# The gated units of a last FFN by one level of Strassen's algorithm: seven half-size products in place of eight

## The chip, the cores and the metric

The kernel runs on one core of a Trainium2 chip. The metric is the device time of one execution in microseconds (us); the time before is the median of three runs. A profiled execution of the same program gives the trace: the instructions of each engine with start and length. The engines are PE (matrix multiplication; PEld is its weight load), DVE (vector), ACT (scalar functions and copies), POOL (the second vector engine) and SP, which issues the DMAs. SBUF is the on-chip memory; PSUM holds PE's sums.

## The reference, cut to what matters

The reference runs two layers over 512 latent tokens, D_MODEL 1024. Layer 0 mixes by latent attention, layer 1 by an S5 state-space layer with a GLU; each is followed by a SwiGLU FFN with 2816 hidden units. Only the last lines of layer 1 matter here: the FFN's input product, its gate, and the output product.

```python
def modulate(x, g, shift, scale):
    return rmsnorm(x, g) * (1 + scale) + shift

def swiglu(h, w_in, w_out):
    a, b = jnp.split(h @ w_in, 2, axis=-1)
    return (jax.nn.silu(a) * b) @ w_out
...
        xl = xl + gt_l * yl
        xl = xl + gt2_l * swiglu(modulate(xl, norm_ffn[i], sh2_l, sc2_l), ffn_w_in[i], ffn_w_out[i])
```

`sh2_l`, `sc2_l` and `gt2_l` are modulation rows, a product of SiLU(c) with `ada_w`.

## The kernel before, in words

**Layout and passes.** Activations stand feature-major: a tile is 128 partitions by KT = 8 chunks of k by 512 tokens. Each fp32 operand is split in two: a high part (`wh` of a weight, `hh` of the data), which ACT copies out in PE's fp32r format (L77), and a low part (`wl`, `hl`), which DVE subtracts (L80). A product is three passes for each k chunk: high by high, high weight by low data, low weight by high data (`passes`, L818).

**The FFN of layer 1** (`ffn(1, …)`, L852 and on). The 2816 hidden units are 22 tiles of 128, called units here. `BLOCKS[1]` puts them in three blocks: units 0 to 7, 8 to 14, 15 to 21. For each unit, `linear` makes two 128 x 512 accumulators, one for a and one for b: 8 chunks by 3 passes of 512 columns each, 48 matmuls in all. ACT makes `sa` = silu(a) (L873), DVE `u` = b x `sa` (L874), and `split` turns u into `uh` (ACT) and `ul` (DVE). Behind the units of a block stand eight output products `fo`, one for each chunk of the output, whose k chunks are the block's units; `residual` (L801, DVE) adds each into x. In the last block x then goes out by DMA.

**Weights.** `stream` issues each weight's DMA some takes ahead (`Stream.take`: depth 4 while the pool `wx1` is open, 2 without it), splits it into `wh` and `wl` and hands it on. A weight tile is 128 x 1024: one half (a or b) of one unit.

**The start.** The second half of the tokens (columns 256 to 511) comes out of the GLU last. Its norm (`Norm.bcast`: PE sums the squares `ss`, L336; DVE and POOL make the reciprocal root `rs` with a power at L308; DVE makes `dg`, L345; PE broadcasts it, `bc`, L346) and its `modulate` stand in the program ahead of the FFN. `modulate` has, for each chunk, a product `hm` on DVE (L353), a scale and shift on ACT, and the split into `hh` (ACT) and `hl` (DVE, every third on POOL). `first1` runs units 0 and 1 as narrow matmuls of 256 columns: the first half of both units (96 matmuls), then the second.

**Modulation rows.** `ada_rows` is a hook called once in a unit: two 128 x 1024 products with a running sum on DVE (L264), for the rows that the output's `residual` needs. It is used up in the first block.

**Order.** Each engine works through its own queue in order. A scheduler lays the queues out from the program's dependencies; instructions passed to `keep_in_program_order` keep the order in which the program writes them. PSUM banks come from the pools that `use_banks(name, two, one)` opens.

## Time and profile before

| | |
|---|---|
| median of three runs | 1765.08 us (1756.75 to 1771.79) |
| profiled execution | 1765.18 us, span 1763.4 us |
| PE busy | 1646.2 us, 93% of the span |
| PEld busy | 1406.3 us, 80% |
| DVE busy | 1077.5 us, 61% |
| ACT busy | 690.8 us, 39% |
| POOL busy | 590.0 us, 33% |

The span is the profiled execution from its first to its last instruction; its own time is 1.8 us longer. Busy shares are means over the whole span. The FFN of layer 1 is the stretch from 1397.1 us to the end.

### The profile page before, as it was taken

The page shows a single profiled execution, that of the slowest core. Times are in us where ns is not written, and L with a number is a line of the kernel's source. Part 1 is how long each engine was busy: PE and PEld are TensorE (multiplying, and loading weights), DVE is VectorE, ACT ScalarE, POOL GpSimd, SP SyncE. Part 2 cuts the span into 40 slices and gives each one's busy share as a digit, 9 for nine tenths or more (in the row PEclk, how much of TensorE's full clock was granted, in tenths as well). Part 3 has the DMA queues.
Part 4 walks back from the last instruction along what each step waited for, and adds up shares of the span by engine and source line. Part 5 has one row for each costly group of instructions (what it writes and reads, how often), then busy time and mean ns, then how long its engine had stood idle before and what let it go on. Part 6 is the DMA issues. An engine that isn't in the chain of part 4 may idle for free. (4 is left out here: it accounts for less than half of the span.)

```text
span 1763.4 us, 29083 instructions
## 1 busy us (share of the span) xinstructions
PE 1646.2 (93%) x11486; PEld 1406.3 (80%) x11486; DVE 1077.5 (61%) x1881; ACT 690.8 (39%) x1400; POOL 590.0 (33%) x626
## 2 busy tenths in 40 slices
PE   6979999999999999999989989976799999999999
PEld 5868878777888887877778878865579988888887
DVE  5787868787997356575566434547965654333332
ACT  3447757677453212222222312246525543232221
POOL 0156454510235247586667300046741100000000
PEclk9999989999999999999999999988879999999999
DMA  9130001124424355566435554353536452333231
GB/s 337 42 119 15 15 12 30 57 81 152 163 85 141 111 176 155 162 195 185 137 117 176 172 203 147 123 180 132 197 123 199 147 175 88 108 91 100 96 88 68
DMA packets 79832, 224.76 MB, mean 127 GB/s; under 512 B 8912, under 2 KB 24144, under 8 KB 77520
## 3 DMA queue, kind: packets, MB, share of 16 engines
q1 hardware_dynamic: 77472, 219.67, 38.4%
q10 hardware_dynamic: 2224, 3.24, 0.5%
q8 instruction: 90, 1.47, 0.3%
q14 instruction: 46, 0.38, 0.1%
HBM read 192.53 MB, written 30.34 MB: 126 GB/s over the span
## 5 line engine op out<-in xcount | busy, mean ns | idle before, releaser
L77 ACT ACTIVATE wh_wi<-wr_wi 128x1024 fp32r<-128x1024 f32 x88 | 93.2, 1061 | 321.6 <-PE f L818 259.5
L80 DVE TENSOR_TENSOR wl_wi<-wr_wi,wh_wi 128x1024 fp32r<-128x1024 f32 x88 | 116.3, 1323 | 130.4 <-ACT wh_wi L77 129.4
L818 PE MATMUL f<-hhh,wl_wi 128*128 128x512 f32 (+1 forms) x704 | 185.5, 341 | 5.0 <-DVE wl_wi L80 5.0
L818 PE MATMUL f<-hhl,wh_wi 128*128 128x512 f32 (+1 forms) x704 | 184.5, 340 | 0.0
L818 PE MATMUL f<-hhh,wh_wi 128*128 128x512 f32 (+1 forms) x704 | 183.7, 340 | 0.1
L818 PE MATMUL fo<-uh,wl_wo 128*128 128x512 f32 (+1 forms) x528 | 161.3, 361 | 9.0 <-DVE wl_wo L80 9.0
L818 PE MATMUL fo<-uh,wh_wo 128*128 128x512 f32 (+1 forms) x528 | 162.7, 364 | 4.3 <-ACT wh_wo L77 2.6
L818 PE MATMUL fo<-ul,wh_wo 128*128 128x512 f32 (+1 forms) x528 | 162.4, 361 | 3.4 <-DVE ul L80 3.4
L326 POOL TENSOR_TENSOR sqa<-sqa,sq 128x256 f32<-128x256 f32 (+2 forms) x25 | 37.9, 1515 | 323.3 <-ACT sq L324 321.5
L77 ACT ACTIVATE wh_wo<-wr_wo 128x512 fp32r<-128x512 f32 (+3 forms) x64 | 50.5, 793 | 239.9 <-PE fo L818 112.7
L818 PE MATMUL f<-hl_f,wh_wi 128*128 128x512 f32 (+1 forms) x384 | 142.8, 372 | 0.0
L818 PE MATMUL f<-hh_f,wl_wi 128*128 128x512 f32 (+1 forms) x384 | 142.6, 372 | 0.0
L818 PE MATMUL f<-hh_f,wh_wi 128*128 128x512 f32 (+1 forms) x384 | 142.1, 372 | 0.0
L801 DVE SCALAR_TENSOR_TENSOR x<-fo,mods,x 128x512 f32<-128x512 f32 x104 | 63.4, 644 | 120.4 <-PE fo L818 120.4
L818 PEld LDWEIGHTS f<-hhh,wl_wi 128*128 128x128 f32 x704 | 109.8, 190 | 21.0 <-DVE wl_wi L80 5.9
L818 PEld LDWEIGHTS f<-hhh,wh_wi 128*128 128x128 f32 x704 | 109.0, 189 | 17.1 <-issue 1.0
L818 PEld LDWEIGHTS f<-hhl,wh_wi 128*128 128x128 f32 x704 | 109.0, 189 | 15.7 <-issue 0.6
L818 PEld LDWEIGHTS fo<-uh,wl_wo 128*128 128x128 f32 x528 | 88.9, 192 | 24.0 <-DVE wl_wo L80 10.0
L818 PEld LDWEIGHTS fo<-uh,wh_wo 128*128 128x128 f32 x528 | 89.3, 193 | 19.7 <-ACT wh_wo L77 3.1
L818 PEld LDWEIGHTS fo<-ul,wh_wo 128*128 128x128 f32 x528 | 89.6, 193 | 18.6 <-DVE ul L80 4.3
L80 DVE TENSOR_TENSOR wl_wo<-wr_wo,wh_wo 128x512 fp32r<-128x512 f32 (+3 forms) x64 | 60.4, 947 | 55.1 <-ACT wh_wo L77 54.9
L709 ACT ACTIVATE pth<-pt 128x384 fp32r<-128x384 f32 (+1 forms) x160 | 71.8, 470 | 42.1 <-PE pt L705 40.7
(401 smaller groups left out, 4033.0 us busy)
## 6 DMA issues: line engine op xcount, KB each, us to landing
wr_wi<-ffn_w_in SPq DMA_DIRECT2D x88, 512.0 KB, 3.7
adaw<-ada_w SPq DMA_DIRECT2D x72, 512.0 KB, 4.5
wr_wg<-s_w_glu SPq DMA_DIRECT2D x30, 512.0 KB, 3.5
adat<-ada_t SPq DMA_DIRECT2D x24, 512.0 KB, 4.9
wr_wmo<-mla_w_o SPq DMA_DIRECT2D x16, 512.0 KB, 3.6
s_wout<-v SPq DMA_DIRECT2D x64, 128.0 KB, 2.6
s_win<-big SPq DMA_DIRECT2D x16, 512.0 KB, 4.8
s5win<-s_win SPq DMA_DIRECT2D x7, 1024.0 KB, 4.8
```

The costliest lines, as they stand in the source:

```text
L77: ins_ = nc.scalar.activation(hi, src, AF.Copy)
L80: eng.tensor_tensor(lo, src, hi.bitcast(F32), ALU.subtract)
L326: nc.gpsimd.tensor_tensor(self.acc, self.acc, sq, ALU.add)
L709: nc.scalar.activation(dh, pt3, AF.Copy)
L801: nc.vector.scalar_tensor_tensor(x[:, m, a:b], acc, gate[:, m, v : v + 1], x[:, m, a:b], op0=ALU.mult, op1=ALU.add)
L818: nc.tensor.matmul(acc, st, xs[lo][:, k, :], start=s, stop=e)
```

## The change

One unit's input product is a matrix of 2 x 2 pieces times a matrix of 2 x 2 pieces: the weights of the a and b halves by the upper and lower four k chunks (`a11`, `a12` for a, `a21`, `a22` for b), and the data by the upper and lower four chunks and the left and right 256 columns (`b11`, `b12`, `b21`, `b22`). Eight products of pieces become seven, of sums of pieces.

- **Weights** (`Ring`): a unit gets seven split operands in 128 x 512 tiles: a11, a12, s1 = a21 + a22, a11' = s1 - a11, a12' = a12 - a11', a21' = a11 - a21, and a22. POOL makes the four sums (L1313, 1316, 1317, 1320), three of them in place over the loaded weight; `done` splits each operand on ACT (L1308) and DVE (L1309). They stand in a ring of nine slots. `steps` hands the work out in pieces, one behind each product of the unit ahead (`todo`).
- **Data**: once, at the start, t1, t2 and t3 and a replaced b12 are made from the modulated `hm` values, which are now kept (`hr`), by four subtractions of 128 x 1024 (two on DVE, two on POOL) and a split each.
- **Products**: `product` is 12 matmuls of 256 columns (four chunks, three passes). `WAYS` lists the seven: which data, which of the four accumulators (y and z in one tile and bank, x and w in another), whether the sum begins anew, and where ACT copies it afterwards (`r` or `q`, 256 columns, L1225). x and z go on summing after they are copied. DVE adds y and z to r (L1229) and x to both halves of q (L1236); ACT applies Silu to r in place (L1232), DVE multiplies r by q (L1237). The split of the result into `uh` and `ul` (L1206, 1207) is put off to behind the first product of the next unit (`tail`).
- **Order**: the instructions of this part on PE, ACT and DVE are pinned to program order. Loads are issued two units ahead, splits one ahead, for the output weights too. The first unit of blocks 1 and 2 is prepared during the last output products of the block ahead.
- **The start**: units 0 and 1 keep the plain product in 256-column halves, but by k halves (`half`); half (0, 0) stands ahead of the second half's `modulate`, half (1, 0), (0, 1) and (1, 1) behind it.
- Units 2 to 21 take the new way: 20 of 22. The output products `fo` stay as they are.

In short, with the core of the new loop:

```diff
         right.close()
-        with pool("ph", side="right") as ph, ExitStack() as wx:
-            more["pool"] = wx.enter_context(pool("wx1"))
...
+            hr = [ph.tile([P, KT, NL // 2], F32, tag="hr", name="hr0")]
+            ring = Ring(nc, pw, split, raw_tile, lambda ht, j: ins["ffn_w_in"][1, ht, j])
...
+            def modulate_half(p_, norm):
+                tiles = [lambda nm, n, k=k: hr[-1][:, k, :] for k in range(KT)]
+                modulate(p_, 3, mod(1, 3), part_of(hh, p_), part_of(hl, p_), norm.bcast(), tiles)
...
+                        if a and m == KT - 2:
+                            ring.load(0)
+                            ring.plain(0)
+                        if a and m == KT - 1:
+                            ring.load(1)
...
-            def first1():
-                abs_ = [accs_for([(0, 0, NL)], f"f1_{i}", 2) for i in range(2)]
-                ws = [[stream.take() for _ in ab] for ab in abs_]
...
-            with pool("pf1") as pf:
-                ffn(1, [(0, 0, NL)], pf, first1, [(hh, hl)], ada_rows(pf, 40, 48, 2))
...
+                quarter = lambda t, k0, c0: (lambda k: t[:, k0 + k, c0 : c0 + NL // 2])
+                pairs_of = lambda k0, c0: (quarter(hh, k0, c0), quarter(hl, k0, c0))
+                b11, b12, b21, b22 = (pairs_of(k0, c0) for k0 in (0, 4) for c0 in (0, NL // 2))
+
+                def product(acc, w, b, start):
+                    for k in range(4):
+                        ws = slice(k * P, (k + 1) * P)
+                        for st, mv in ((w[0], b[0]), (w[0], b[1]), (w[1], b[0])):
+                            pin(nc.tensor.matmul(acc, st[:, ws], mv(k), start=start and k == 0 and st is w[0] and mv is b[0],
+                                                 stop=(k == 3 and st is w[1]), skip_group_check=True))
...
+                def half(i, h):
+                    ws = ring.parts.pop(i) if h else ring.parts[i]
+                    for j in range(2):
+                        for kh in range(2):
+                            product(wide[i][j][:, h * 256 : h * 256 + 256], ws[2 * j + kh], pairs_of(4 * kh, 256 * h), kh == 0)
+
+                half(0, 0)
+                modulate_half(HALVES[1], norms[1])
+                half(1, 0)
+                t1, t2, t3 = (pair_tile(f"t{j}") for j in range(3))
+                view = lambda t: [t[:, lo].rearrange("p a (b c) -> p (a b) c", b=2) for lo in range(2)]
+                t1, t2, t3 = view(t1), view(t2), view(t3)
+                h0, h1 = hr
+                top, low = slice(0, 4), slice(4, 8)
+                nc.vector.tensor_sub(h0[:, top], h1[:, top], h0[:, top])
+                nc.gpsimd.tensor_tensor(h1[:, top], h1[:, low], h1[:, top], ALU.subtract)
+                nc.vector.tensor_sub(h1[:, low], h1[:, low], h0[:, top])
+                nc.gpsimd.tensor_tensor(h0[:, low], h0[:, low], h1[:, low], ALU.subtract)
+                half(0, 1)
+                todo = prepare_unit(0)
+
...
+                for t, raw in ((t1, h0[:, top]), (t2, h1[:, low]), (t3, h1[:, top])):
+                    split(t[0], t[1], raw)
+                    next(todo, None)
+                plain_gate(0)
+                next(todo, None)
+                half(1, 1)
+                split(hh[:, top, NL // 2 :], hl[:, top, NL // 2 :], h0[:, low])
+                for _ in todo:
+                    pass
+                plain_gate(1)
+                tq = lambda t: tuple((lambda k, z=z: z[:, k, :]) for z in t)
+
+                WAYS = [(b11, "x", True, ("r", 0)), (b21, "y", True, None), (tq(t1), "z", False, ("q", 1)),
+                        (tq(t2), "x", False, ("r", 1)), (b22, "z", False, None), (tq(t3), "x", False, None),
+                        (b12, "w", False, ("q", 0))]
+                two = lambda t: t.rearrange("p (a b) -> p a b", a=2)
+                tail = None
+                V = nc.vector
+
+                def done(r, ht, b0, hi, lo):
+                    pin(nc.scalar.activation(hi[:, ht - b0, :], r, AF.Copy))
+                    pin(V.tensor_sub(lo[:, ht - b0, :], r, hi[:, ht - b0, :].bitcast(F32)))
...
+                use_banks("psum_f", 1, 6)
+                for n, (bi, ht, _) in enumerate(units):
+                    b0, b1 = BLOCKS[1][bi]
+                    load_unit(n + 2)
+                    todo = prepare_unit(n + 1)
+                    if ht >= 0:
+                        if ht == b0:
+                            uh, ul = new_u(bi)
+                        yz, xw = ps1(f"fyz_{ht}"), ps1(f"fxw_{ht}")
+                        at = {"y": yz[:, 0:256], "z": yz[:, 256:512], "x": xw[:, 0:256], "w": xw[:, 256:512]}
+                        r, q = unit_tiles(ht)
+                        for i, (b, acc, start, to) in enumerate(WAYS):
+                            product(at[acc], ring.parts[ht][i], b, start)
+                            if to:
+                                t = {"r": r, "q": q}[to[0]]
+                                pin(nc.scalar.activation(t[:, 256 * to[1] : 256 * to[1] + 256], at[acc], AF.Copy))
+                            if i == 0 and tail:
+                                done(*tail)
+                            if i == 4:
+                                pin(V.tensor_add(r, yz, r))
+                            next(todo, None)
+                            if i == 4:
+                                pin(nc.scalar.activation(r, r, AF.Silu))
+                        for _ in todo:
+                            pass
+                        ring.parts.pop(ht)
+                        pin(V.tensor_add(two(q), at["x"].unsqueeze(1).to_broadcast([P, 2, 256]), two(q)))
+                        pin(V.tensor_mul(r, r, q))
+                        tail = r, ht, b0, uh, ul
+                        next(rows, None)
+                    else:
...
+                        if m == 0 and bi == 0:
+                            assert next(rows, None) is None
+                            rows_pool.close()
+                            ring.extra = late.enter_context(pool("late"))
+                        if b1 < HT and m == 4:
+                            ring.load(b1, True)
+                            early = ring.steps(b1)
+                        if b1 < HT and m >= 6:
+                            for _ in range(3 if m == 6 else 4):
+                                next(early, None)
+                        for _ in todo:
+                            pass
+                        acc = [ps1(f"fo1_{bi}_{m}")]
+                        linear(acc, ahead_.pop(n), [(uh, ul)], b1 - b0)
+                        residual(acc[0], (0, 0, NL), m, mod(1, 5))
+                        if b1 == HT:
+                            nc.sync.dma_start(outs["out"][:, m, :], x[:, m, :NL])
     banks.close()
...
+    def load(self, ht, extra=False):
+        if extra:
+            self.raw[ht] = [self.extra.tile([P, 1024], F32, tag=f"raw{j}", name=f"wr1_{ht}_{j}") for j in range(2)]
+        else:
+            tags = ("w_hi", "w_lo") if ht % 2 else ("w_raw", "w_raw")
+            self.raw[ht] = [self.raw_tile(t, f"wr1_{ht}_{j}") for j, t in enumerate(tags)]
+        for j in range(2):
+            self.nc.sync.dma_start(self.raw[ht][j], self.src(ht, j))
+
...
+    def steps(self, ht):
+
+        a11, a12, a21, a22 = self.quarters(ht)
+        out = self.parts[ht] = []
+        G = self.nc.gpsimd
+
+        def done(q):
+            out.append(self.slot())
+            hi, lo = out[-1]
+            self.pin(self.nc.scalar.activation(hi, q, AF.Copy))
+            self.pin(self.nc.vector.tensor_sub(lo, q, hi.bitcast(F32)))
+
+        done(a11)
+        s1 = self.pool.tile([P, 4 * P], F32, tag="s1", name=f"s1_{ht}")
+        G.tensor_tensor(s1, a21, a22, ALU.add)
+        yield
+        done(a12)
+        G.tensor_tensor(a21, a11, a21, ALU.subtract)
+        G.tensor_tensor(a11, s1, a11, ALU.subtract)
+        yield
+        done(s1)
+        G.tensor_tensor(a12, a12, a11, ALU.subtract)
+        yield
+        for q in (a11, a12, a21, a22):
+            done(q)
+            yield
```

How the order moves, at three places. In the names, the digits before the last underscore are the unit or, for `wh` and `wl` after, the ring's count.

On ACT in the first block, before, a turn of one unit was four instructions (the Silu of one unit, the copy of u, two weight copies of 128 x 1024); two turns stand here:

```order
L873 ACTIVATE sa_10_16027<-f_10_0_15966 128x512
L77 ACTIVATE uh_1_15830<-u_10_16028 128x512
L77 ACTIVATE wh_wi_13_0_16064<-wr_wi_13_0_15934 128x1024
L77 ACTIVATE wh_wi_13_1_16101<-wr_wi_13_1_15971 128x1024
L873 ACTIVATE sa_11_16094<-f_11_0_16033 128x512
L77 ACTIVATE uh_1_15830<-u_11_16095 128x512
```

After, one unit's turn on ACT (unit 11's products, with unit 10's `uh` and the weight copies of unit 12):

```order
L1225 ACTIVATE r_11_16696<-fxw_16695 128x256
L1206 ACTIVATE uh_1_16289<-r_10_16561 128x512
L1308 ACTIVATE wh_79_16713<-wr_12_0_16555 128x512
L1308 ACTIVATE wh_80_16731<-wr_12_0_16555 128x512
L1225 ACTIVATE q_11_16697<-fyz_16694 128x256
L1308 ACTIVATE wh_81_16750<-s_12_16717 128x512
L1225 ACTIVATE r_11_16696<-fxw_16695 128x256
L1308 ACTIVATE wh_82_16768<-wr_12_0_16555 128x512
L1308 ACTIVATE wh_83_16785<-wr_12_0_16555 128x512
L1232 ACTIVATE r_11_16696<-r_11_16696 128x512
L1308 ACTIVATE wh_84_16802<-wr_12_1_16556 128x512
L1225 ACTIVATE q_11_16697<-fxw_16695 128x256
```

The copy of u stood ahead of the weights' copies; now `uh` stands between two copies out of PSUM, and the copy of z to q (the fifth row) stands behind it and two weight copies.

On DVE, before, two units (the product u, its low part, two weight subtractions of 128 x 1024):

```order
L874 TENSOR_TENSOR u_8_15894<-f_8_0_15832,sa_8_15893 128x512
L80 TENSOR_TENSOR ul_1_15831<-u_8_15894,uh_1_15830 128x512
L80 TENSOR_TENSOR wl_wi_11_0_15931<-wr_wi_11_0_15802,wh_wi_11_0_15930 128x1024
L80 TENSOR_TENSOR wl_wi_11_1_15968<-wr_wi_11_1_15837,wh_wi_11_1_15967 128x1024
L874 TENSOR_TENSOR u_9_15961<-f_9_0_15899,sa_9_15960 128x512
L80 TENSOR_TENSOR ul_1_15831<-u_9_15961,uh_1_15830 128x512
```

After, one unit (from unit 10's product r x q to unit 11's):

```order
L1237 TENSOR_TENSOR r_10_16561<-r_10_16561,q_10_16562 128x512
L1207 TENSOR_TENSOR ul_1_16290<-r_10_16561,uh_1_16289 128x512
L1309 TENSOR_TENSOR wl_79_16714<-wr_12_0_16555,wh_79_16713 128x512
L1309 TENSOR_TENSOR wl_80_16732<-wr_12_0_16555,wh_80_16731 128x512
L1309 TENSOR_TENSOR wl_81_16751<-s_12_16717,wh_81_16750 128x512
L1309 TENSOR_TENSOR wl_82_16769<-wr_12_0_16555,wh_82_16768 128x512
L1229 TENSOR_TENSOR r_11_16696<-fyz_16694,r_11_16696 128x512
L1309 TENSOR_TENSOR wl_83_16786<-wr_12_0_16555,wh_83_16785 128x512
L1309 TENSOR_TENSOR wl_84_16803<-wr_12_1_16556,wh_84_16802 128x512
L1309 TENSOR_TENSOR wl_85_16820<-wr_12_1_16556,wh_85_16819 128x512
L1236 TENSOR_TENSOR q_11_16697<-fxw_16695,q_11_16697 128x512
L1237 TENSOR_TENSOR r_11_16696<-r_11_16696,q_11_16697 128x512
```

What was four instructions in a unit is eleven of 512 columns, in one fixed order; the subtractions from `wl_81` on read sums that POOL makes. POOL has no instruction in this stretch before; after, one unit is four:

```order
L1313 TENSOR_TENSOR s_12_16717<-wr_12_1_16556 128x512
L1316 TENSOR_TENSOR wr_12_1_16556<-wr_12_0_16555,wr_12_1_16556 128x512
L1317 TENSOR_TENSOR wr_12_0_16555<-s_12_16717,wr_12_0_16555 128x512
L1320 TENSOR_TENSOR wr_12_0_16555<-wr_12_0_16555 128x512
```

The last three write in place over the loaded weights, each from an earlier sum or piece.

On PE at the start, before, the broadcast of the second half's norm stood among the narrow matmuls of unit 1:

```order
L818 MATMUL f_1_0_14915<-hh_f_13797,wh_wi_1_0_14816 128x256
L818 MATMUL f_1_0_14915<-hl_f_13798,wh_wi_1_0_14816 128x256
L818 MATMUL f_1_0_14915<-hh_f_13797,wl_wi_1_0_14817 128x256
L818 MATMUL f_1_0_14915<-hh_f_13797,wh_wi_1_1_14916 128x256
L818 MATMUL f_1_0_14915<-hl_f_13798,wh_wi_1_1_14916 128x256
L346 MATMUL bc_256_14863<-dg_256_14864,ones 128x128 x2
L818 MATMUL f_1_0_14915<-hh_f_13797,wl_wi_1_1_14917 128x256
```

After, it stands directly behind the sums of squares, between unit 0's first half and unit 1's:

```order
L1138 MATMUL f_0_0_14881<-hh_f_13797,wh_4_14776 128x256
L1138 MATMUL f_0_0_14881<-hl_f_13798,wh_4_14776 128x256
L1138 MATMUL f_0_0_14881<-hh_f_13797,wl_4_14777 128x256
L336 MATMUL ss_256_14931<-ones,sqa_256_13801 128x1 x2
L336 MATMUL ss_256_14931<-ones,sq_256_6_14785 128x1 x2
L336 MATMUL ss_256_14931<-ones,sq_256_7_14845 128x1 x2
L346 MATMUL bc_256_14941<-dg_256_14942,ones 128x128 x2
L1138 MATMUL f_1_0_14882<-hh_f_13797,wh_5_14857 128x256
L1138 MATMUL f_1_0_14882<-hl_f_13798,wh_5_14857 128x256
```

PE now comes to the broadcast with nothing between it and the sums that DVE and POOL have to answer.

## Rows read from the trace of the kernel before

**Rows 1.** Windows: us, PE, PEld, DVE, ACT, POOL busy, PE clock, DMA share, GB/s

```profile
1397.10:1422.10 25.00, 25.00 (x211) 24.90 (x210) 9.79 (x22) 11.08 (x22) 2.19 (x3) 1.00 0.14 43
1422.10:1487.40 65.30, 65.30 (x291) 54.09 (x290) 34.47 (x45) 21.81 (x29) 0.00 (x0) 1.00 0.52 169
...
1530.90:1607.10 76.20, 76.20 (x338) 63.16 (x337) 25.27 (x27) 21.27 (x27) 0.00 (x0) 1.00 0.31 91
```

**Rows 2.** Chain that ended last: start, us, engine, tile, line, instructions

```profile
1531.05 76.16 PE f L818 x336
1607.21 38.08 PE fo L818 x168
```

**Rows 3.** PE timeline, narrow and wide matmuls: start, us, engine, line, operation

```profile
1402.79 0.28 PE L818 MATMUL f<-hl_f,wh_wi 128*128 128x256 f32 x1
...
1403.15 0.28 PE L818 MATMUL f<-hl_f,wh_wi 128*128 128x256 f32 x1
...
1403.51 0.50 PE L336 MATMUL ss<-ones,sq 128*128 128x1 f32 x4
1403.87 0.36 PE L818 MATMUL f<-hl_f,wh_wi 128*128 128x256 f32 x1
...
1530.89 0.39 PE L818 MATMUL f<-hh_f,wh_wi 128*128 128x512 f32 x1
...
1531.57 0.39 PE L818 MATMUL f<-hh_f,wh_wi 128*128 128x512 f32 x1
```

**Rows 4.** ACT timeline, in the GLU and in one gated unit

```profile
1380.88 0.37 ACT L1079 ACTIVATE sg<-gl 128x256 f32<-128x256 f32 x1
...
1454.70 1.06 ACT L77 ACTIVATE wh_wi<-wr_wi 128x1024 fp32r<-128x1024 f32 x1 [4.37 <-PE f L818]
1455.67 0.58 ACT L873 ACTIVATE sa<-f 128x512 f32<-128x512 f32 x1
1457.65 0.63 ACT L77 ACTIVATE uh<-u 128x512 fp32r<-128x512 f32 x1 [1.41 <-DVE u L874]
```

**Rows 5.** DVE timeline, the same gated unit

```profile
1456.94 0.68 DVE L874 TENSOR_TENSOR u<-f,sa 128x512 f32<-128x512 f32 x1
1458.32 0.69 DVE L80 TENSOR_TENSOR ul<-u,uh 128x512 fp32r<-128x512 f32 x1 [0.70 <-ACT uh L77]
1458.93 1.22 DVE L264 SCALAR_TENSOR_TENSOR adat<-adat,ada_c 128x1024 f32<-128x1024 f32 x1
```

**Rows 6.** POOL timeline, an addition with DVE at other work

```profile
732.71 1.30 POOL L1267 TENSOR_TENSOR v<-ot,ot 128x512 f32<-128x512 f32 x1
```

**Rows 7.** POOL timeline, beside DVE's rows of the next group

```profile
701.47 2.03 POOL L1262 TENSOR_TENSOR ot<-gr,hr 128x384 f32<-128x384 f32 x1
703.45 1.86 POOL L1263 TENSOR_TENSOR ot<-gi,hi 128x384 f32<-128x384 f32 x1
...
706.48 1.15 POOL L1265 TENSOR_TENSOR ot<-gr,hi 128x384 f32<-128x384 f32 x1
...
1377.12 1.03 POOL L80 TENSOR_TENSOR hl_f<-hm,hh_f 128x256 fp32r<-128x256 f32 x1 [2.57 <-ACT hh_f L77]
```

**Rows 8.** DVE timeline, beside POOL's rows and once alone (723.18)

```profile
701.27 1.22 DVE L80 TENSOR_TENSOR wl_wi<-wr_wi,wh_wi 128x1024 fp32r<-128x1024 f32 x1
...
702.60 1.71 DVE L80 TENSOR_TENSOR ul<-u,uh 128x768 fp32r<-128x768 f32 x1
...
723.18 0.96 DVE L80 TENSOR_TENSOR ul<-u,uh 128x768 fp32r<-128x768 f32 x1
...
1377.47 0.48 DVE L1081 SCALAR_TENSOR_TENSOR gz<-gl,mods,sg 128x256 f32<-128x256 f32 x1
```

**Rows 9.** DVE timeline, modulation of the second half

```profile
1405.03 0.48 DVE L345 TENSOR_SCALAR dg<-packed,rs 128x128 f32<-128x128 f32 x2 [0.82 <-POOL rs L308]
1408.31 1.42 DVE L353 TENSOR_TENSOR hm<-x,bc 128x256 f32<-128x256 f32 x4 [2.80 <-PE bc L346]
...
1415.01 0.76 DVE L80 TENSOR_TENSOR hl_f<-hm,hh_f 128x256 fp32r<-128x256 f32 x2 [1.15 <-ACT hh_f L77]
```

142 lines of the change are left out of this document (103 added, 39 removed).

## Prediction

> **What bounds the kernel now.** I read the page's busy shares first (PE 93% of the span), then the stretch that the change touches, then its chain. From 1397.1 us, where the GLU ends, to the last output product PE is busy all the time: 65.30 us of 65.30 in the gated units of the first block, 76.20 of 76.20 in those of the second, granted clock 1.00, the 2.4 GHz level, while DVE and ACT are busy for a half to a quarter of it and POOL not at all [rows 1]. The chain that ended last runs through PE there, without a gap: 76.16 us for seven gated units, 38.08 for the eight output products behind them [rows 2]. So one gated unit costs 76.16 / 7 = 10.88 us, and whatever the change takes from PE's matmuls comes off the end until another engine makes PE wait. Which one is near that is the question, since the change gives ACT, DVE and POOL more to do.
>
> **The matmuls.** Four 512-column matmul starts span 0.68 us for three, 0.2267 each; 256-column ones 0.36 for three, 0.120 each [rows 3]. A unit was 48 wide matmuls, 48 x 0.2267 = 10.88 us. It becomes seven products of four k by three passes, 84 narrow ones: 84 x 0.120 = 10.08 us, a product 1.44. An eighth of the columns goes, but half of a wide matmul would be 0.113 and a narrow one is 0.120, which eats 6% again. Twenty units (2 to 21; units 0 and 1 keep their narrow halves, and the output products are the same) give 20 x 0.80 = **16.0 us, 0.91%**: the most that this can bring.
>
> **What the other engines get.** An operation frees its engine about 0.09 us before its row ends: the next starts 0.97 after a 1.06 us one on ACT, 0.61 after a 0.69 us one on DVE [rows 4, 5]. So I count 0.54 for a 512-wide copy on ACT (row 0.63), 0.28 for a 256-wide one out of PSUM (nearest row: sg, 0.37), 0.49 for Silu, and 0.60 for a 512-wide DVE operation (0.68 and 0.69, from PSUM or not) [rows 4, 5]. A unit that also prepares the next one's seven weight sums then has on ACT 8 x 0.54 + 4 x 0.28 + 0.49 = 5.9 us, on DVE 11 x 0.60 = 6.6, on POOL four 512-wide additions of 1.30 us [rows 6], with a 0.07 gap 5.5. Each alone fits in 10.08.
>
> They don't fit side by side. Where a POOL operation meets a DVE operation that reads two SBUF tiles, one waits for the other's end. DVE's wl_wi runs from 701.27 to 702.49, and POOL's 384-wide product that begins at 701.47 takes 2.03 us in place of 1.15 [rows 7, 8]. DVE's 768-wide subtraction, issued at 702.60, ends at 704.31, 1.71 us in place of 0.96, and the next POOL row waits in its turn (1.86) [rows 7, 8]. The subtraction's 0.75 us of waiting ends at about 703.35, 0.15 before POOL's row does; so a 1.30 us POOL row holds DVE off for about 1.16. An operation with one input in PSUM isn't held: gz at 1377.47 takes its 0.48 while a POOL row is under way [rows 7, 8].
>
> The Trainium skill (SBUF — State Buffer, section Who interferes with whom) states this as a rule: a DVE instruction with two SBUF inputs contends with a GpSimd instruction that reads SBUF, and the second to issue waits for the whole of the first. The trace agrees, by the rows above. By the rule's opposite, engines that don't disturb each other, the sum would be the first rival's.
>
> Nine of the eleven DVE operations of a unit read two SBUF tiles (seven wl, ul, the product r x q): 9 x 0.60 = 5.4 us, and POOL's four hold 4 x 1.16 = 4.6 us more. That is 10.0 of 10.08 us, with no wait in between; and there are waits, since the order of ACT and DVE is fixed.
>
> **The loop.** From the product r x q of one unit (t = 0 on DVE) to that of the next, with 0.04 us from an end to the start that waits for it (uh ends at 1458.28, ul starts at 1458.32) [rows 4, 5]: uh on ACT 0.72 to 1.35; behind it the first wh of the next unit, done 1.89; DVE's ul from 1.38, wl(1) from 1.98, wl(2) from 2.58. POOL's third sum needs wl(1), wants the port at 2.7, gets it after wl(2) at 3.18, ends 4.48. wl(3) is held to 4.34 and ends its hold at 4.94; POOL's fourth sum from 4.94 to 6.24. wh(4), of POOL's third sum, is done at 5.15; wl(4) is held to 6.10, then 6.70. The sum r (one SBUF input) 6.70 to 7.30, while POOL takes s for the unit after: wl(5) is held to 7.86, 8.46; POOL's next one again, wl(6) held to 9.62, 10.22; wl(7) 10.82; q from PSUM 11.42; the product at 11.5. **11.5 us a turn, and no PE in it**: more than PE's new 10.08, and more than the old 10.88. PE feels it at the fifth product: it writes z again after ACT has copied z to q, and that copy stands on ACT behind uh and two wh, about 2.1 us after the product r x q. This wait is new; before, no PE wait stands in this stretch.
>
> The first unit of a block has no uh ahead of its copies, so PE keeps its own pace for two units, and half of the third's delay shows; I take 10.08, 10.08, 11.0 and three times 11.5 for the six preparing units of the second and the third block, 65.7 us against 65.3: +0.4 each. The last unit of each of the three blocks prepares nothing: 10.08, -0.8 each.
>
> In the first block two 1024-wide products of the modulation rows stand between r x q and ul in three units, and once ahead of unit 2. They were there before, where PE hid them. Now they delay ul, and so wl(1), from 1.38 to 0.60 + 2 x 1.14 = 2.88 [rows 5]: a turn is 13.0. With the start's delay handed on I take 13.2 for its five preparing units: 5 x (13.2 - 10.88) = +11.6.
>
> **The start.** The first narrow halves and their count stay. Before, the sums of squares and the broadcast stood among them; now PE issues the three sums and at once the broadcast, which waits for DVE and POOL: from ss to the end of dg 2.0 us (1403.51 to 1405.51) [rows 3, 9]. Some 2.5 us for the group against four inserts of 0.36 [rows 3]: +1.1. Then the second half of unit 0 reads all eight chunks of hh in two products, 2.9 us, where it took them over 5.8. It begins 5.8 us after the broadcast and wants the last chunk at 8.3; before, the last hl was done 7.5 after the first hm (1408.31 to 1415.77) [rows 9]. Now eight multiplications (0.33 each), a 1024-wide subtraction and a 1024-wide split stand ahead of the last hl on DVE, 7.0 us in all, with POOL's subtraction (twice 1.16) and one hl holding the port for 2.9 and a wait for ACT's 7.4 us of copies: near 11.5, 3.2 late. Start: +4.3. The bounds of this are 0 (ACT done first, as before) and +7 (the port fully alternating).
>
> **What costs nothing.** Weight loads are issued two units ahead instead of four; the DMA share is a third of the stretch [rows 1], and a load has a unit's 10 us to land. The split of an output weight waits one product longer, 4.76 us, for about 2.3 us of work. Before the GLU's second half no instruction moves.
>
> **Sum.** -2.4 (last units) + 0.8 + 11.6 + 4.3 = +14.3 us. On the profiled execution's own 1765.2 us, which is the median of the three runs to 0.1 us, that makes **1780 us, 0.8% slower**. About 1% is what a measurement of this kernel tells from no change, so this counts as within 1%, near its upper edge.
>
> **Rivals.** *The hold is hidden* (DVE and POOL miss each other, or a held operation has slack). Without holds the same turn is 9.3 us: POOL's third sum at 2.70, its fourth to 5.37, wl(7) at 8.6, q 9.3. PE bounds again: -16.0, the start +3.2, the rows about +2.2: 1754.6 us, 0.6% faster. For it: the two holds need POOL's sums to fall where the loop puts them, and a queue's order can drift into a better phase. Against it: the port's 10.0 of 10.08 us leaves nearly no phase that fits.
> *The sums on POOL take longer than 1.30* and the loss is over 1%. Four of POOL's operations lie in the turn, so 0.1 us more in each adds 0.4 to a turn, over some 12 turns 5 us. The row of 1.30 is of the same kind, undisturbed [rows 6]; where POOL adds in place and ACT and the loads are busy it could be 1.45: +7 us, 1787 us. It decides from 1.37 us on, where the sum passes 17.7.
> *The change doesn't do what it says*: the built order has 1680 narrow matmuls more and 960 wide ones fewer, 20 x 84 and 20 x 48; so it does.
>
> **How the numbers follow.** Forecast 0.54 (1770 to 1783 for it alone), hold hidden 0.22 (1750 to 1770), POOL longer 0.24 (1783 to 1797). Faster by over 1% would need the whole 16 us and more: 0.06. Slower by over 1%: the third case and a part of the first, 0.31. The rest, 0.63, is within 1%. The range leaves a tenth out at each end: 1753 to 1792.
>
> **What would show it.** PE's pieces of 84 matmuls at 0.120; in each preparing unit one gap ahead of the fifth product, released by ACT's copy to q, of 1.4 us in the later blocks and 3 to 5 in the first; POOL rows of 1.7 to 2.3 us beside DVE rows over 1.2; the units of the second block 10.1 us at its head and 11.5 at its end. If POOL's rows stay at 1.3 and PE shows no gap, the hold was the wrong step; if the gaps are released by POOL or a load, the loop was.

## The result, and the profile after

The changed kernel takes 1788.52 us (1785.37 to 1791.72), the kernel before in the same rounds 1763.44: a ratio of 1.0139, with a 95% interval of 1.0108 to 1.0171. It is slower by 25 us where 14.3 were forecast. The time lies in the range, though near its upper end, and the direction is right. The mechanism that the forecast rests on stands in the trace: a turn of the loop takes 11.34 us where 11.5 were forecast. But the term for the last units of the blocks has the wrong sign.

The profiled execution (1785.37 us, span 1783.6) has PE's last GLU matmul end 5.6 us sooner than that of before, at 1391.7 us. The GLU itself takes 105.6 us in both, and in runs 3 and 5 below, whose edits come later in the program, its end stands at 1391.5 and 1400.0 us; so this point varies from one execution to the next. I therefore count from there: 366.1 us to the end before, 391.9 after, 25.8 more. First the windows view of the changed kernel, cut at the start, the three blocks' gated units and the output products behind each. Columns: us, then busy time of PE, PEld, DVE, ACT and POOL (instructions), granted clock, DMA share, GB/s.

```profile
1391.50:1421.50 30.00, 26.77 (x211) 26.51 (x210) 22.45 (x29) 15.91 (x31) 18.58 (x11) 0.94 0.17 59
1421.50:1502.90 81.40, 69.06 (x519) 67.23 (x518) 70.40 (x84) 37.40 (x75) 33.54 (x21) 0.94 0.38 117
1502.90:1545.60 42.70, 41.91 (x181) 33.44 (x181) 20.62 (x23) 11.13 (x15) 3.22 (x2) 1.00 0.29 93
1545.60:1624.40 78.80, 74.46 (x600) 72.65 (x599) 66.83 (x70) 40.99 (x84) 42.36 (x26) 1.00 0.30 94
1624.40:1662.60 38.20, 36.99 (x161) 29.35 (x160) 19.82 (x23) 10.49 (x15) 4.00 (x3) 1.00 0.30 92
1662.60:1744.30 81.70, 77.37 (x608) 75.77 (x607) 62.82 (x70) 41.03 (x84) 37.56 (x24) 0.98 0.26 80
1744.30:1783.60 39.30, 34.83 (x151) 27.56 (x149) 14.36 (x17) 6.62 (x8) 0.00 (x0) 0.99 0.30 100
```

Where [rows 1] have PE busy for 65.30 of 65.30 and 76.20 of 76.20 us, PE now idles 12.3 us in the first block's units and 4.3 in each of the others. POOL, idle there before, is busy for 33 to 42 us, and DVE for 63 to 70 in place of 25 to 34. The granted clock, 1.00 in [rows 1], is 0.94 in the start and the first block.

Next the chain that ended last, one turn of the second block (start, us, engine, tile, line). In [rows 2] this was one piece of 76.16 us on PE.

```profile
1584.65 1.62 POOL wr L1317
...
1586.29 0.64 ACT wh L1308
...
1586.96 1.55 DVE wl L1309
...
1590.39 2.15 DVE wl L1309 x2
1592.54 0.61 DVE q L1236
...
1593.17 0.70 DVE r L1237
...
1593.90 0.64 ACT uh L1206
...
1596.00 1.62 POOL wr L1317
```

PE is not in it. The chain goes from POOL's third sum (L1317) through ACT's copy and DVE's subtractions to q, r x q, uh, and back to POOL's third sum 11.35 us later. POOL's timeline of the same turn (start, us, engine, line, operation, and in brackets the idle time ahead and what ended it):

```profile
1584.65 1.61 POOL L1317 TENSOR_TENSOR wr<-s,wr 128x512 f32<-128x512 f32 x1 [4.62 <-DVE wl L1309]
1586.34 1.63 POOL L1320 TENSOR_TENSOR wr<-wr 128x512 f32<-128x512 f32 x1
1587.92 1.75 POOL L1313 TENSOR_TENSOR s<-wr 128x512 f32<-128x512 f32 x1
```

DVE's timeline beside it:

```profile
1585.05 1.76 DVE L1309 TENSOR_TENSOR wl<-s,wh 128x512 fp32r<-128x512 f32 x1
1586.96 1.55 DVE L1309 TENSOR_TENSOR wl<-wr,wh 128x512 fp32r<-128x512 f32 x1
1588.43 0.68 DVE L1229 TENSOR_TENSOR r<-fyz,r 128x512 f32<-128x512 f32 x1
1589.04 1.19 DVE L1309 TENSOR_TENSOR wl<-wr,wh 128x512 fp32r<-128x512 f32 x1
1590.39 2.15 DVE L1309 TENSOR_TENSOR wl<-wr,wh 128x512 fp32r<-128x512 f32 x2 [0.16 <-ACT wh L1308]
1592.46 0.68 DVE L1236 TENSOR_TENSOR q<-fxw,q 128x512 f32<-128x512 f32 x1
1593.17 0.69 DVE L1237 TENSOR_TENSOR r<-r,q 128x512 f32<-128x512 f32 x1
```

And PE's, the matmuls with a wait ahead of them:

```profile
1573.21 0.38 PE L1138 MATMUL fyz<-hh_f,wh 128*128 128x256 f32 x1 [1.00 <-ACT q L1225]
...
1584.54 0.38 PE L1138 MATMUL fyz<-hh_f,wh 128*128 128x256 f32 x1 [1.00 <-ACT q L1225]
...
1595.89 0.39 PE L1138 MATMUL fyz<-hh_f,wh 128*128 128x256 f32 x1 [1.02 <-ACT q L1225]
```

POOL's rows take 1.61 to 1.75 us where the undisturbed one takes 1.30 [rows 6]. DVE's subtractions wl, 0.69 when nothing holds them ([rows 5] have 0.69 for the like), take 1.76 and 1.55 beside them, while the sum r, with one input in PSUM, keeps its 0.68 at 1588.43 beside a POOL row. PE waits once a turn, ahead of the fifth product, for ACT's copy to q, and the turns are 11.33 and 11.35 us.

The second thing in the trace was not forecast. It lies around the last units of each block; here the chain in unit 6, the last but one of the first block:

```profile
1475.36 1.19 DVE wl L1309
...
1476.57 3.48 DMA wr_wo<-ffn_w_out
...
1480.07 1.06 ACT wh_wo L77
...
1482.69 0.28 ACT q L1225
...
1483.01 2.93 PE fyz L1138 x12
```

ACT's timeline at the same place:

```profile
1480.07 1.06 ACT L77 ACTIVATE wh_wo<-wr_wo 128x1024 fp32r<-128x1024 f32 x1 [2.32 <-DMA wr_wo<-ffn_w_out]
1481.03 0.61 ACT L1206 ACTIVATE uh<-r 128x512 fp32r<-128x512 f32 x1
1481.55 1.13 ACT L1308 ACTIVATE wh<-wr 128x512 fp32r<-128x512 f32 x2
1482.59 0.36 ACT L1225 ACTIVATE q<-fyz 128x256 f32<-128x256 f32 x1
```

ACT stands for 2.32 us on the load of the first output weight. That copy (wh_wo) stands in ACT's queue ahead of uh, two weight copies and the copy to q, so PE idles for 3.52 us ahead of its fifth product, which starts at 1483.01, and the clock is down. Windows of that stretch and of a whole turn of the second block:

```profile
1482.90:1489.00 6.10, 5.99 (x28) 6.00 (x29) 5.95 (x7) 2.85 (x7) 5.11 (x4) 0.50 0.30 86
1573.20:1584.54 11.34, 10.33 (x84) 10.13 (x84) 10.28 (x12) 6.22 (x14) 6.56 (x4) 1.00 0.00 1
```

Behind the 3.5 us gap the granted clock is 0.50 (1.2 GHz) for these 6.1 us, and a narrow matmul takes 0.212 us in place of 0.120; behind the gaps of 1.0 us it is 1.00.

### The profile page after: what moved, and what is told of

Read it like the earlier page. It is cut to its first block, busy times and chain, and to the rows that moved or that the text cites. A ratio compares the mean times of both kernels' runs of the same rounds, so it can differ in the third digit from the quotient of the medians.

```text
span 1783.6 us, 30985 instructions
## 1 busy us (share of the span) xinstructions
PE 1638.4 (92%) x12206; PEld 1428.1 (80%) x12206; DVE 1220.5 (68%) x2031; ACT 756.7 (42%) x1588; POOL 727.5 (41%) x708
## 5 line engine op out<-in xcount | busy, mean ns | idle before, releaser
L77 ACT ACTIVATE wh_wi<-wr_wi 128x1024 fp32r<-128x1024 f32 x44 | 46.7, 1061 | 187.6 <-PE f L818 165.1
L1309 DVE TENSOR_TENSOR wl<-wr,wh 128x512 fp32r<-128x512 f32 x120 | 117.9, 1010 | 9.7 <-ACT wh L1308 8.4
L818 PEld LDWEIGHTS fo<-uh,wl_wo 128*128 128x128 f32 x528 | 88.5, 191 | 25.7 <-DVE wl_wo L80 11.8
L1317 POOL TENSOR_TENSOR wr<-s,wr 128x512 f32<-128x512 f32 x20 | 31.6, 1582 | 169.3 <-DVE wl L1309 169.2
L1308 ACT ACTIVATE wh<-wr 128x512 fp32r<-128x512 f32 x120 | 72.1, 622 | 46.9 <-POOL wr L1317 27.5
L80 DVE TENSOR_TENSOR wl_wi<-wr_wi,wh_wi 128x1024 fp32r<-128x1024 f32 x44 | 62.6, 1422 | 35.7 <-ACT wh_wi L77 35.7
L710 DVE TENSOR_TENSOR ptl<-pt,pth 128x384 fp32r<-128x384 f32 (+1 forms) x160 | 80.3, 520 | 8.2 <-ACT pth L709 7.7
```

What stands on the lines that cost most here:

```text
L77: ins_ = nc.scalar.activation(hi, src, AF.Copy)
L80: eng.tensor_tensor(lo, src, hi.bitcast(F32), ALU.subtract)
L710: nc.vector.tensor_sub(dl, pt3, dh.bitcast(F32))
L818: nc.tensor.matmul(acc, st, xs[lo][:, k, :], start=s, stop=e)
L1308: self.pin(self.nc.scalar.activation(hi, q, AF.Copy))
L1309: self.pin(self.nc.vector.tensor_sub(lo, q, hi.bitcast(F32)))
```

## The experiments

Ratios are to the kernel before, run in the same rounds. "The start" is the time from PE's first matmul behind the GLU to unit 2's first product: 24.9 us before, 30.0 after. "From the GLU's end" is the time from PE's last GLU matmul to the end of the profiled execution, 366.1 us before and 391.9 after.

**1. The holds, taken away (e1_psum_lo).** Seven of the nine DVE operations with two SBUF inputs in a unit, the subtractions wl, get one input in PSUM: a tile of zeros in place of the high part. The kernel leaves the right low parts out; it is there for its time alone.

```diff
-            self.pin(self.nc.vector.tensor_sub(lo, q, hi.bitcast(F32)))
+            self.pin(self.nc.vector.tensor_sub(lo, q, hi.bitcast(F32) if self.zero is None else self.zero))
...
+                ring.zero = ps2("zero")[:, :512]
+                nc.vector.memset(ring.zero, 0.0)
```

> Leaves out part of the computation: the low parts of the weights' sums of units 3 to 21 subtract a PSUM tile of zeros in place of the high part, so that seven of a unit's nine DVE operations with two SBUF inputs read one SBUF tile and one PSUM tile; their number, size and order stay. Theory 1 (DVE and POOL hold each other off): the turn in the second and third block falls from 11.34 us to PE's 10.08, no gap ahead of the fifth product there, POOL's sums 1.3 us each in place of 1.62 and 1.75; in the first block, with the modulation rows, 11.5 in place of 13. About 13 us less than the changed kernel, near 1775. Theory 2 (the fixed order over three engines is too long by itself, the holds matter little): turn 11.2 to 11.4 as before, gaps of 1.0 us stay, 1785 to 1790.

Measured: 1766.44 us, ratio 1.0005 (0.9988 to 1.0022). Nearly six units of the second block in its windows view:

```profile
1544.80:1604.30 59.50, 59.50 (x496) 59.45 (x495) 40.76 (x63) 38.41 (x76) 28.86 (x23) 1.00 0.24 70
```

POOL's timeline in one of them:

```profile
1573.50 1.30 POOL L1320 TENSOR_TENSOR wr<-s,wr 128x512 f32<-128x512 f32 x1 [4.75 <-DVE wl L1312]
```

And DVE's at the same time:

```profile
1573.84 0.68 DVE L1312 TENSOR_TENSOR wl<-s,zero 128x512 fp32r<-128x512 f32 x1
1574.83 0.69 DVE L1312 TENSOR_TENSOR wl<-wr,zero 128x512 fp32r<-128x512 f32 x1 [0.31 <-POOL wr L1320]
```

PE is busy all the time, 59.50 of 59.50 us, at 10.08 a unit. POOL's sums take 1.30, DVE's subtractions 0.68 beside them. No gap ahead of a fifth product is left, not even in the first block with its modulation rows. The time is 9 us below what Theory 1 gave, though unit 2 here waits 6.2 us for unit 1's gate (DVE's r, L1182, which reads PSUM), probably since the zeros take PSUM from the same pool: the start is 36.4 us. Theory 2 falls, unless the subtractions gained because they no longer wait for ACT.

**2. The control (e5_sbuf_lo).** The same subtractions with a constant in SBUF. It leaves out the same part.

```diff
+                self.pin(self.nc.vector.tensor_sub(four(lo), four(q), self.ones.unsqueeze(1).to_broadcast([P, 4, P])))
```

> Leaves out the same part as the run with PSUM zeros: the low parts of the weights' sums of units 3 to 21 subtract a constant in place of the high part, here one that lies in SBUF. Nothing else differs from that run: the subtractions wait for no high copy in either. Theory 1 (two SBUF inputs hold POOL off and are held): all of the changed kernel's turn comes back, 11.2 to 11.4 us in the second block, POOL's sums 1.6 to 1.8 us, about 1785. Rival (the run with PSUM zeros was fast since its subtractions no longer wait for ACT): 10.08 us, no gap, POOL's sums 1.3 us, 1760 to 1767.

Measured: 1791.48 us, ratio 1.0144 (1.0110 to 1.0178). DVE's timeline in one turn:

```profile
1599.24 1.78 DVE L1315 TENSOR_TENSOR wl<-s,ones 128x512 fp32r<-128x512 f32 x1
```

And POOL's:

```profile
1598.89 1.58 POOL L1323 TENSOR_TENSOR wr<-s,wr 128x512 f32<-128x512 f32 x1 [4.64 <-DVE wl L1315]
1600.55 1.62 POOL L1326 TENSOR_TENSOR wr<-wr 128x512 f32<-128x512 f32 x1
1602.13 1.74 POOL L1319 TENSOR_TENSOR s<-wr 128x512 f32<-128x512 f32 x1
```

The turn is 11.33 again, with the same gap of 1.0 us, though no subtraction waits for a high copy. Where no POOL sum is under way, two of these subtractions in a row take 1.28 us (at 1598.04), so the form of the constant, a 128-column tile read four times, costs nothing by itself. The two runs differ in where one input lies, and by 25 us: the hold is the cause. DVE and POOL take turns, a 0.68 us subtraction held to 1.78, a 1.30 us sum to 1.58 to 1.74. The Trainium skill (SBUF — State Buffer, section Who interferes with whom) states this: outside its two-port modes, a DVE instruction with at most one SBUF input doesn't contend with GpSimd (POOL), and one with two SBUF inputs contends with a GpSimd instruction that reads SBUF. The trace agrees, with 0.68 against 1.78.

**3. The sums on DVE (e2_dve_sums).** All four weight sums move from POOL to DVE; the last three are changed like the first.

```diff
-        G = self.nc.gpsimd
+        G = self.nc.vector
...
-        G.tensor_tensor(s1, a21, a22, ALU.add)
+        self.pin(G.tensor_tensor(s1, a21, a22, ALU.add))
```

> The four weight sums of a unit move from POOL to DVE, pinned where the program writes them. Theory 1 (holds): a sum costs DVE 0.60 us and no longer holds it off for 1.2 and more; 15 operations of 0.60 and 0.8 of waiting for uh are 9.8 us, under 10.08: no gap in the second and third block, 12.1 in place of 13 in the first. About 1775. Theory 2 (the chain is too long anyway): DVE gets 2.4 us more in a turn that has 11.34, POOL's 1.6 leave it: 12.1 us a turn, some 10 us slower than the changed kernel, near 1798.

Measured: 1781.18 us, ratio 1.0095 (1.0071 to 1.0119): 7 us less than the changed kernel with 2.4 us more work a turn on DVE, and from the GLU's end 383.2 us in place of 391.9. But the turn is 11.0, not 9.8. DVE has 15 operations of 0.60 in it, 9.1 us; it waits 0.70 for uh (at 1598.61), 0.68 for the sixth high copy (at 1595.11), which stands on ACT behind Silu, and 0.1 when an operation reads what the one before it wrote. Neither theory's number came; Theory 1's sum had missed ACT's order.

**4. The modulation rows, later (e3_rows_late).**

```diff
-                    next(rows, None)
+                    if ht == 0:
+                        next(rows)
...
+                            if ht == 7 and i >= 3:
+                                next(rows)
...
-                        next(rows, None)
```

> The four pairs of modulation rows move from units 1 to 4 to the later products of unit 7, which prepares no weights. Theory 1 (rows stand in the loop's DVE queue): units 3 to 6 fall from 12.5 to 13.6 us to 11.4, unit 2 comes 2 us sooner, and the low clock behind the long gaps goes in part: 7 to 9 us less than the changed kernel, near 1780. Rival (the first block is slow from its start's delay and late loads): gaps of 2.5 us stay, within 2 us of the changed kernel. Rival (the rows' loads, two at a time, now delay unit 7's own sums): 3 to 5 us come back in the wait ahead of the first output products.

Measured: 1788.38 us, ratio 1.0140 (1.0111 to 1.0169): no change. The turns of units 3 to 5 did fall to 11.3 us, as in the second block, and units 2 to 6 took 59.4 us in place of 68.5. But the rows now stand ahead of unit 7's own q on DVE, the last four products each waiting for its load, 5.4 us in all, and PE waits for that unit's uh, as its timeline ahead of the output products shows:

```profile
1511.53 0.80 PE L818 MATMUL fo<-uh,wh_wo 128*128 128x512 f32 x1 [7.25 <-ACT uh L1207]
```

From unit 7's first product to the end of the first output stretch it takes 63.9 us in place of 55.6, so 8.3 of the 9.2 us come back. The second rival was right in kind and too small in size.

**5. The output weights' copies, pinned (e4_wo_pinned).**

```diff
                     else:
+                        stream.pinned = True
                         ahead_[n] = halve(ahead_[n])
```

> The high copies of the output weights are pinned in program order on ACT, so that the first of a block stands in the block's last unit and no longer ahead of uh in the unit before, where it waited 2.3 us for its load. Theory 3 (the late load holds ACT, the copy to q stands behind it, and PE's gap takes the clock down): the gap of 3.5 us at unit 6 falls to 1 to 2.5, that of 1.8 at unit 20 to 1.0, and the low clock behind them goes: 5 to 7 us less than the changed kernel, near 1782. Rival (the wait is only moved): the output products wait for their copies instead, gaps of 2 us at the head of each output stretch, no more than 2 us less.

Measured: 1782.33 us, ratio 1.0094 (1.0065 to 1.0124), 6 us less than the changed kernel; from the GLU's end 383.2 us in place of 391.9. PE's timeline at the place of the 3.5 us gap:

```profile
1490.39 0.39 PE L1139 MATMUL fyz<-hh_f,wh 128*128 128x256 f32 x1 [1.43 <-ACT q L1226]
1490.61 0.28 PE L1139 MATMUL fyz<-hl_f,wh 128*128 128x256 f32 x1
```

The gap is 1.43, and behind it the clock is not down: the second matmul has 0.28, where at 1.2 GHz it had 0.42. The gap at unit 20 is 1.0. Unit 6 takes 11.8 us in place of 16.5, unit 20 11.3 in place of 13.6. The output products wait 0.7 to 0.8 us, once behind the first block and twice behind the second. Theory 3 holds for the load and ACT's queue. Its clock part holds at these two places, but behind unit 5's gap of 2.5 us, where the clock was 1.00 in the changed kernel, it is 0.50 here, and unit 5 takes 14.1 us in place of 12.8.

**6. Sums on DVE in a new order (e6_tuned).** Two sums fill DVE's wait for uh, Silu stands behind the sixth copy, one modulation row a unit, output weights' copies pinned.

```diff
-                rows = ada_rows(rows_pool.enter_context(pool("rows1")), 40, 48, 2)
+                rows = ada_rows(rows_pool.enter_context(pool("rows1")), 40, 48, 1)
...
+                            if i == 0 and more_units:
+                                next(todo, None)
                             if i == 0 and tail:
                                 done(*tail)
...
-                            next(todo, None)
-                            if i == 4:
+                            if more_units or i > 2:
+                                next(todo, None)
+                            if i == 5:
                                 pin(nc.scalar.activation(r, r, AF.Silu))
...
+        pin(V.tensor_tensor(s1, a21, a22, ALU.add))
+        pin(V.tensor_tensor(a21, a11, a21, ALU.subtract))
+        yield
         done(a11)
...
+        pin(V.tensor_tensor(a11, s1, a11, ALU.subtract))
         yield
         done(a12)
...
+        pin(V.tensor_tensor(a12, a12, a11, ALU.subtract))
```

> The sums on DVE, with the first two of a unit put between the product r x q and ul, Silu on ACT behind the sixth high copy in place of the fourth, one modulation row a unit in place of two (the last two in unit 7), and the output weights' high copies pinned. Theory 1 and 3: DVE's turn is 15 x 0.605 and 0.1 to 0.3 of waiting, 9.3 us, 10.4 with a row: no gap in the second and third block, gaps under 0.5 in the first, the low clock there gone, the start as it is: about 27 us less than the changed kernel in these stretches, near 1763, the kernel before within 4 us. Theory 2 (the chain over three engines is too long in any order): turn 10.8 and more, 1778 to 1782 as with the sums on DVE alone.

Measured: 1758.88 us, ratio 0.9964 (0.9942 to 0.9986): less than both kernels, by 0.4% against the one before. In the second and third block no gap is left. In the first, where a row still stands in each turn, the turns are 11.1 with gaps of this kind on PE, more than the 0.5 us expected:

```profile
1455.57 0.39 PE L1139 MATMUL fyz<-hh_f,wh 128*128 128x256 f32 x1 [0.77 <-ACT q L1227]
```

The run changes four things at once. Run 3 has one of them by itself and run 5 another; what the order of the sums and of Silu brings alone was not measured.

**7. The rows into the GLU (e8_tuned_rows).** Run 6, with the modulation rows one behind every other chunk of the GLU.

```diff
+                rows = ada_rows(pr, 40, 48, 1)
+                next(rows)
...
                         norm.add(m, x[:, m, a:b])
+                        if m % 2 == 0:
+                            next(rows)
```

> The kernel with sums on DVE and the new order, and the eight modulation rows moved out of the first block into the GLU, one behind every other chunk. If the rows are what is left in the first block (gaps of 0.93 to 1.06 us ahead of the fifth product of units 3 to 6), those gaps and the waits at that block's last unit go: 4 to 5 us less than that kernel, near 1754. Rival (the GLU's DVE and DMA have no room): the GLU's 86 us grow by as much, the same time within 2 us.

Measured: 1755.47 us, ratio 0.9950 (0.9934 to 0.9967), the lowest of all, though the interval overlaps that of run 6. The windows view of five units' length of the first block:

```profile
1440.00:1490.00 50.00, 50.00 (x411) 49.70 (x411) 42.50 (x67) 29.58 (x58) 0.00 (x0) 1.00 0.22 68
```

No gap is left behind the start. From the GLU's end it has 357.0 us, 9 less than before. Of the new way's 16.0 us, 15.7 are there behind the start; the start takes 6.6 back. In the GLU PE now idles for 5.1 us in place of 3.0, so the rows aren't free there: against run 6 the profile gains 5.2 us from the GLU's end, and the medians differ by 3.4.

**8. The start, three ways.** e9_tuned_cover and e7_tuned_start build on run 6, e10_tuned_rows_k on run 7, e11_kmajor on the changed kernel. e9 and e7 put half of unit 1's first products ahead of the broadcast (cut); e7 besides moves all four data subtractions to DVE, behind half (0, 1).

```diff
                 half(0, 0)
+                norms[1].sums()
+                half(1, 0, (0,))
                 modulate_half(HALVES[1], norms[1])
-                half(1, 0)
+                half(1, 0, (1,))
```

> The kernel with sums on DVE and the new order, with one change at the start: half of unit 1's first narrow products stand between the sums of squares and the broadcast; the data subtractions stay where they are. If PE's wait for the broadcast costs the start what the trace shows (1.7 to 2.1 us of gap, the low clock behind it 1.3), 2 to 3.5 us less than that kernel and a start of 27 us in place of 29.9. Rival (the start is set by ACT and DVE behind the broadcast, which now comes later or at the same time): the start stays at 30, the same time within 1 us; the wait only moves to the last low parts.

> The kernel with sums on DVE and the new order, and the start besides: half of unit 1's first narrow products stand between the sums of squares and the broadcast, the four data subtractions are all on DVE and behind half (0, 1) in program order. If the start's 5 us are PE's wait for the broadcast (2.1 us and the low clock behind it, 1.4) and POOL and DVE holding each other off ahead of the last low parts (1.9), 4 to 5 us less than without this, near 1759, some 0.3% faster than the kernel before. Rival (DVE's own work of some 21 us in a start of 25 is the limit): the wait ahead of unit 2 grows by as much, no more than 2 us less.

e10 and e11 make both products of each k chunk before the next chunk:

```diff
-                    for j in range(2):
-                        for kh in range(2):
-                            product(wide[i][j][:, h * 256 : h * 256 + 256], ws[2 * j + kh], pairs_of(4 * kh, 256 * h), kh == 0)
+                    for kh in range(2):
+                        for k in range(4):
+                            for j in range(2):
...
```

> The fastest kernel so far (sums on DVE, new order, modulation rows in the GLU) with the narrow halves of units 0 and 1 by chunks again: for each of the eight k chunks both products, as the kernel before had it, so that the last chunk of the modulated second half is wanted 5.1 us after the first and no longer 1.3. If the start's 5 to 6.5 us are in part PE reading all chunks at once, the gap of 2.2 us ahead of the low part from POOL goes, 2 us less, 1753 to 1754. Rival (unit 2's operands, t1 above all, set the start): the gap moves to unit 2's third product, within 1 us of 1755.5.

> The changed kernel with that one edit alone, the narrow halves by chunks. By the same reasoning 2 us of its start of 30.0 us at most; its first block's gaps then begin earlier or grow by as much, since DVE and POOL are behind there: 1786 to 1789.

Measured: e9 1761.87 us, ratio 0.9987 (0.9970 to 1.0004), start 32.8. e7 1763.09, 0.9979 (0.9956 to 1.0002), start 32.1. e10 1757.05, 0.9970 (0.9952 to 0.9988), start 29.1. e11 1788.04, 1.0130 (1.0089 to 1.0171), start 28.2. In none does the time fall clear of noise. In three of them a gap that goes comes back at a later thing that PE reads. With the broadcast's wait covered, the last low part from POOL is later still, here on PE in e9:

```profile
1415.87 0.58 PE L1147 MATMUL f<-hl_f,wh 128*128 128x256 f32 x1 [3.24 <-POOL hl_f L80]
```

With that gap closed by chunk order, unit 2's fourth product waits, here on PE in e10:

```profile
1440.58 0.50 PE L1144 MATMUL fxw<-t,wh 128*128 128x256 f32 x2 [1.29 <-ACT r L1235]
```

In e11 unit 2 takes 15.2 us in place of 13.2, and its start is 1.8 us shorter. For these three the rivals had it. e7 is another case: PE idles 2.7 us in its start against run 6's 3.2, but the granted clock is 0.50 for 6.8 us of it in place of 3.4. The clock is also at 0.50 for 6.8 us in the starts of e8, e9 and e10, so some 1.7 us of each of these starts, by half of the 3.4 us more, is the clock's; with one profile each I can't tell whether the edits bring that. What the start's floor is made of (ACT's 16 scalings and copies, the four data subtractions and splits on DVE) was not taken apart further, and stays open.

## Why the prediction was right or wrong

**The matmuls** were right: a product 1.44 us, a unit without a wait 10.08. The 16.0 us are real, as run 7 shows, and run 1 in its second block.

**The hold** was right, in kind and size, and runs 1 and 2 show it: 1.16 us for a full hold was forecast, 1.07 to 1.10 measured (1.76 and 1.78 against 0.69 and 0.68). **The loop** was right as a path: it closes without PE, and PE has one wait in it, at the fifth product, released by the copy to q, 1.0 us long where I had 1.4. That its length came so near, 11.34 us for 11.5, is in part luck. By the DVE rows above (1.76, 1.55 and 1.19 against 0.69, and 2.15 for a pair against the 1.29 of an undisturbed one) four holds of a turn come to 3.3 us, where the loop had 4.0; DVE's waits for ACT's high copies, some 0.5 us a turn, were not in it.

**The modulation rows** were right as a delay: 13.0 us a turn forecast, 12.8 to 13.0 measured from one r x q to the next in the three turns that hold them. Units 2 to 6 took 68.5 us (1421.5 to 1490.0), 14.1 more than the 54.4 of before, forecast +11.6; what is over is unit 6, which took 16.5 us with the load's wait and the low clock behind it.

**The start** was forecast at +4.3 and came to +5.0 (30.0 against 24.9), but by other terms. PE's waits in it:

```profile
1400.14 1.11 PE L346 MATMUL bc<-dg,ones 128*128 128x128 f32 x4 [1.45 <-DVE dg L345]
...
1411.80 0.39 PE L1138 MATMUL f<-hl_f,wh 128*128 128x256 f32 x1 [1.78 <-POOL hl_f L80]
```

The sums and the broadcast take 3.6 us of PE's time against 1.9 before, +1.7 where I had +1.1; the last low part is 1.8 us late where I had 3.2; and the low clock behind the broadcast's wait costs the other 1.5, which I had put at nothing. The near number is luck.

**The failed step** is "the last unit of each of the three blocks prepares nothing: 10.08, -0.8 each", with "what costs nothing" under it: weight loads two units ahead with "a unit's 10 us to land", and the split of an output weight with one product more than enough. From the last units' first product to the end of the output stretch the blocks took +1.2, +2.0 and +0.7 us (55.6 against 54.4, 50.9 against 49.0, 53.7 against 53.0), forecast -0.8 each: 6.3 of the 11.5 us that the sum was short. The same wait for an output weight's load stands in units 6 and 20, one unit earlier; it accounts for the 2.5 us by which units 2 to 6 were over, and for the 1.6 us by which the third block's units were. The DMA share that I called a third is 0.52 in the first block [rows 1]. The load can't start two units ahead: it needs a buffer that a unit's raw weights still hold, and it starts at 1476.57, when DVE's last read of that half ends. The scheduler had put that weight's copy on ACT a unit too early, ahead of uh, since only the loop's own instructions were pinned. The order of ACT that I followed was unit 11's; I did not follow it at units 6 and 20.

Run 5 shows this cause for units 6 and 20, where 4.7 and 2.3 us go. In the last stretches it takes back 0.7, 0.9 and 1.3 us and leaves 55.0, 50.0 and 52.4: there the output products still wait for their weights' copies, in the first two. In run 7, which also has the sums on DVE, the new order and the rows elsewhere, the three stretches take 53.6, 48.4 and 52.2, the forecast's -0.8 within 0.3 us. So a last unit does gain what I forecast where nothing of the output weights or of DVE's queue holds it; how much of the rest is each one's share is open.

**The chances.** I gave 0.63 to a change within 1% and 0.31 to a loss of more; the second came. The rival with longer sums on POOL had the nearest number, 1787, but not the cause: undisturbed, POOL's in-place sums take 1.30 (run 1), and what lengthens them is the hold that the forecast already counted. A loss of 25 us came from that hold, as forecast, together with the output weights' late copies, which no rival had, and a start near the forecast one.

## What to carry to other kernels

An operation that moves from DVE to POOL to relieve DVE doesn't relieve it where DVE's own operations have two SBUF inputs: a 0.60 us addition on DVE became a 1.30 us one that held DVE off for up to 1.1. Count a turn's two-input operations on DVE and POOL as one engine's, before choosing where a sum goes. One input in PSUM took the holds away in run 1, which was no complete kernel; where it fits, it is worth a try. In a loop whose queues are fixed by hand, follow the turn through every queue to itself, and look at the first and last turn by themselves: there an unpinned neighbour's copy and its late buffer stood ahead of the loop's own work.

## What the runs showed that I had not expected

A DVE operation that reads what the one before it wrote starts 0.71 to 0.73 us after it, not 0.60 (q at 1592.46 and r x q at 1593.17 in the changed kernel). An order that keeps such pairs apart is worth about 0.1 us a pair.

PE's clock fell behind some gaps and not behind others: 0.50 behind the 3.5 us one at 1483, 1.00 behind the 2.5 us one at 1469 (granted clock from 1460.7 to 1473.6). The length of the gap doesn't settle it. Unit 5 has a gap of 2.51 us ahead of its fifth product in the changed kernel and in run 5; these are the windows behind it, the changed kernel first:

```profile
1469.10:1472.00 2.90, 2.84 (x23) 2.85 (x24) 2.87 (x7) 0.80 (x3) 1.03 (x1) 1.00 0.54 117
...
1477.30:1480.20 2.90, 2.84 (x13) 2.84 (x14) 2.87 (x7) 0.80 (x3) 1.02 (x1) 0.50 0.41 117
```

In the same time PE starts 23 matmuls in the one and 13 in the other. What decides between the two is open. By the windows of the changed kernel, with 0.94, 0.94 and 0.98, PE ran some 17 us at half speed (each 0.01 below 1.00 is 2% of the stretch at half speed), which cost it 8 us at most. No term of the forecast had it.
